# Cache copies and last intermediate stores of a transformer block, moved from GpSimd's DMA queue to ScalarE's and SyncE's

## The chip, the core and the metric

The kernel runs on one core of a Trainium2 chip. The core has TensorE (matrix products), VectorE, ScalarE and GpSimd (elementwise work), SyncE (which here only issues transfers), and DMA engines that move data between the chip's DRAM, the on-chip SBUF and so on. TensorE writes its products to PSUM, a small memory in banks from which the other engines drain them. Each engine takes its instructions from its own queue in order. A transfer is issued by an instruction in the queue of SyncE, ScalarE or GpSimd. The metric is device time in microseconds for one execution, as a median over runs; lower is better.

## The reference

The kernel computes one block of a network on 1056 tokens (1024 of a prompt, 32 of eight sampled sequences) of width 1024, in float32: a feed forward, a mixer (a convolution branch and a windowed attention with caches, merged by gates), and a second feed forward, each added to its input. Cut to what matters here:

```python
# D_MODEL 1024, D_FF 2816, L = 1
xp = xp + 0.5 * swiglu_ffn(rmsnorm(xp, ffn1_norm[l]), ffn1_w_in[l], ffn1_w_out[l])
...                                   # mixer: adds merge_branches(...)
xp = xp + 0.5 * swiglu_ffn(rmsnorm(xp, ffn2_norm[l]), ffn2_w_in[l], ffn2_w_out[l])
# the same for xs; for each of three windows, 128, 512 and 2048:
kf = jnp.concatenate([cache_k[g][l], ks[:, :, hsl]], axis=1)   # old rows, then four new ones
new_k_s[g].append(kf[:, kf.shape[1] - keep_s:])                # an output; the same for v
```

Outputs are the tokens, and the new caches. Most of a new cache is the old cache, shifted by the new rows, so a large part of the outputs is a plain copy from DRAM to DRAM.

## The kernel before

Activations lie transposed, with features on the partitions and tokens along the free axis. Each float32 product is taken in three TensorE passes over parts of 12 bits, so each operand is split in a high part (`wh`, a ScalarE copy, L170) and a low part (`wl`, the difference, by VectorE or GpSimd, L171). L164 to L172 hold this.

The second feed forward has two stages. In the hidden stage, the first two of 22 tiles of 128 hidden features are done plainly, and 20 by `hidden_fast`, which takes seven products of 24 matmuls each for one tile, in the Winograd form of Strassen's product. For one tile, SyncE loads two blocks of weights (`wr`), VectorE forms four sums of them (L433 to L436, into a `quad` buffer), each sum or block is split, and the seven products drain from PSUM into the same quad, by ScalarE (for instance L473, L476) or VectorE. There are four PSUM buffers for it, two per product. At a tile's end VectorE and ScalarE form the activation (L459, L462, L463), and `hidden_pair` follows: tiles 2i and 2i+1 are a pair, and for each of two token halves the kernel stores the operands that the second stage wants (combinations of the two tiles, by GpSimd, L517 and L522 to L524) to DRAM arrays `hx`. A quad is one of five buffers in a ring, so a later tile's sums wait until an earlier tile's store has been read out.

In the second stage, `ffn_out_fast` multiplies by the output weights, again in seven products for each of three groups of pairs; it loads weights (L563) and operands `hx` (L592), forms sums of weights (L569), and adds products to the tokens.

The order of instructions comes from two sources. The program has a clock that ticks once per block of matmuls; `later(n, fn)` has `fn` called n ticks on. Then a planner of the framework orders the instructions of each engine by a simulated machine. `keep_in_program_order` pins an instruction behind the one last traced on its engine.

`copy_caches` issues DRAM-to-DRAM copies of caches this way. Its part 0 (18 copies) is called in the first feed forward and issues from ScalarE. Its part 1 (17 copies) is called ahead of the second hidden stage with `COPY2 = (17, 7)`: the first copy comes 17 blocks of matmuls later, and then one each seven blocks, which is one per hidden tile. These are issued from GpSimd. No instruction waits for a copy's data. The stores of `hidden_pair` go out from SyncE, but for those of the last pair, four of them, which go out from GpSimd (`ENDQ = 1`).

Of the kernel before, what the change touches and what calls it, by code (L numbers as in the profile page):

```python
# [20 lines left out]
T = TP + TS  # L21
NB = 3
BW = T // NB
DFF = 2816
# [7 lines left out]
# which of the splits (by tile) VectorE takes, GpSimd the others  # L32
# [4 lines left out]
# places in the program, in blocks of matmuls: first, distance  # L37
# [4 lines left out]
ENDQ = 1  # L42
# [19 lines left out]
class Kern:  # L62
    """Activations are kept transposed (features on partitions, the 1056 tokens along the free axis). A float32 product
    x * w is taken in three float32r passes: x = xh + xl and w = wh + wl exactly, with 12 bits in each part."""
# [34 lines left out]
    def after(self, ins, first):  # L99
        """ins is issued after first (whose tile has its place by then)"""  # L100
        self.tc.add_manual_dep(ins.ins, first.ins.name, mybir.DependencyInfo(mybir.DependencyClass.NoSync, mybir.DependencyReason.DATA),
                               reason="order")

    def in_order(self, n0):
        """the instructions since n0 keep their order on each engine"""
        last = {}
        for i in self.nc.cur_bb.bb.instructions[n0:]:
            if i.engine == mybir.EngineType.SP:
                continue
            if i.engine in last:  # L110
                self.tc.add_manual_dep(i, last[i.engine].name, mybir.DependencyInfo(mybir.DependencyClass.NoSync, mybir.DependencyReason.DATA),
                                       reason="order")
            last[i.engine] = i
# [30 lines left out]
    def weights(self, src, kt, n, eng=None):  # L144
        """src: DRAM [kt*128, n] -> kt pairs (hi, lo) [128, n]"""
        nc = self.nc
        raw = self.P.tile([128, kt, n], F32, name=self.nm("wr"), tag="wr", bufs=3)
        nc.sync.dma_start(out=raw, in_=src.rearrange("(k p) n -> p k n", p=128))
        w = []
        for k in range(0, kt, 512 // n):  # L150
            m = min(512 // n, kt - k)
            hi = self.P.tile([128, m, n], F32R, name=self.nm("wh"), tag="wh", bufs=6)
            lo = self.P.tile([128, m, n], F32R, name=self.nm("wl"), tag="wl", bufs=6)
            nc.scalar.activation(hi, raw[:, k:k + m, :], AF.Copy)  # L154
            (eng or nc.gpsimd).tensor_tensor(out=lo, in0=raw[:, k:k + m, :], in1=f(hi), op=ALU.subtract)  # L155
            w += [(hi[:, j, :], lo[:, j, :]) for j in range(m)]
        return w

    def gemm(self, ps, w, xs, tb, tick=True):
        """ps[:, :BW] = sum_k w[k]^T xs[k][:, tb]"""  # L160
        nk = len(xs)
        for k, ((hi, lo), (xh, xl)) in enumerate(zip(w, xs)):
            for i, (p, x) in enumerate(((hi, xh), (hi, xl), (lo, xh))):
                self.nc.tensor.matmul(ps[:, :BW], p, x[:, blk(tb)],  # L164
                                      start=(k == 0 and i == 0), stop=(k == nk - 1 and i == 2))
        if tick:
            self.tick()
# [24 lines left out]
    def load_x(self, gname):  # L192
        """x^T (also to DRAM) and its norm, by blocks"""
# [85 lines left out]
    def norm_rows(self):  # L279
        """the normalized input of a feed forward, in float32 and split"""  # L280
        q = [self.quad() for _ in range(2)]
        self.hf = [q[k // 4][:, k % 4, :] for k in range(KT)]
        self.hs = [(self.hrow(), self.hrow()) for _ in range(KT)]
# [29 lines left out]
    def norm_feed(self, gname, k, tb):  # L313
        """after the last change of x^T's tile k in block tb; rbn gathers the squares' sums"""
        nc = self.nc
        if self.hn[k] is None:
            self.hn[k] = (self.hrow(), self.hrow())
        self.scaled(gname, k, tb, self.hn)
        self.square(k, tb)

    def norm_end(self, cols):
        """1/rms: rb over the tokens along the free axis, cols over tokens on partitions"""
# [16 lines left out]
    def hidden(self, w_in):  # L339
        """2 * silu(gate) * up -> self.hd, for 128 hidden features at a time"""  # L340
# [9 lines left out]
    def hidden_plain(self, g0, u0, g1, u1):  # L350
        """the first two tiles, from the normalized input as it comes by blocks"""
# [34 lines left out]
    # Winograd's form of Strassen's product, on [gate; up] x [first, second half of the features] and  # L386
    # [first, second half of the features] x [first, second half of the tokens]: 7 products in place of 8.
    #   S1 = A21 + A22   S2 = S1 - A11   S3 = A11 - A21   S4 = A12 - S2
    #   T1 = B12 - B11   T2 = B22 - T1   T3 = B22 - B12   T4 = T2 - B21
    #   P1 = A11 B11  P2 = A12 B21  P3 = S4 B22  P4 = A22 T4  P5 = S1 T1  P6 = S2 T2  P7 = S3 T3  # L390
    #   U2 = P1 + P6   U3 = U2 + P7   U4 = U2 + P5
    #   C11 = P1 + P2   C12 = U4 + P3   C21 = U3 - P4   C22 = U3 + P5
# [21 lines left out]
    def combine_last(self):  # L414
        """T4, in the place of B12"""
# [88 lines left out]
    # The same form for the output projection: [even, odd tiles of hidden features] x [first, second half of the tokens].  # L504
    # B11, T1, B21, B22, T3, T2, T4 of a pair of tiles go to self.hx.
# [3 lines left out]
    def hidden_pair(self, j, b, C):  # L509
# [10 lines left out]
        else:  # L520
# [4 lines left out]
            eng = nc.gpsimd if i >= DFF // 256 - ENDQ else nc.sync  # L525
            eng.dma_start(out=self.hx[i][1][:, :, sl], in_=C)
            eng.dma_start(out=self.hx[i][2][:, 0, sl], in_=k[:, b])

    def hidden_pair0(self, b):
        """from the two plain tiles"""  # L530
# [15 lines left out]
    def ffn_out_fast(self, w_out, final):  # L546
        """x^T += half of w_out^T hidden^T"""
# [9 lines left out]
        def load_w(c, q):  # L557
            """A11, A12, A21, A22: by two output tiles each"""
# [12 lines left out]
        def sums(c):  # L571
            """S2 in the place of A11, S1 in that of A21"""
# [7 lines left out]
        def last_sum(c):  # L580
            """S4, in the place of A12"""
            a = A[c]
            a["P3"] = a["P2"] if c < len(PAIRS) - 1 else block()
            combine(c, a["P3"], a["P2"], a["P6"], ALU.subtract)
# [85 lines left out]
    def ffn_out(self, w_out, after, begin=None):  # L670
        """x^T += half of w_out^T hidden^T, self.hd in chunks"""
# [39 lines left out]
    def store_y(self, o, h):  # L711
        """y for output tile o and half h of the tokens"""
# [52 lines left out]
    def u_unit(self, i):  # L765
        """u^T for 128 conv channels, and the conv's work on it, queued"""
# [29 lines left out]
        def states():  # L796
            # the last 32 prompt tokens and the sample tokens, for the conv states
# [6 lines left out]
            # sample tokens behind their states  # L804
# [31 lines left out]
    def conv_norm(self):  # L836
        """LayerNorm over channels and 2 * silu, split -> self.ca"""
# [62 lines left out]
    def gcols(self, row, g, i):  # L900
        """columns, in group g's order, of the prompt tokens 128 i + 0..127: by residue"""
# [11 lines left out]
    def keep(self, kind, g, i, src):  # L913
        """rows of k or v that are outputs"""
# [49 lines left out]
    def pack_sample(self):  # L964
        """the sample tokens' two parts, side by side"""
# [16 lines left out]
    def v_post(self, g, i, m, ps):  # L982
        """v in the order of the group's keys"""
# [74 lines left out]
    def attn_scores(self, g, i, keys, QT, KTt, V):  # L1058
# [6 lines left out]
        # the two heads of a pair on row tiles of their own, so in banks of their own  # L1065
# [56 lines left out]
    def merge(self, i):  # L1122
        """the three groups' parts, by their softmax sums -> b_attn^T"""
# [43 lines left out]
    def keep_sample(self, g):  # L1167
        """the sample tokens' q^T, k^T and v of this group"""
# [7 lines left out]
    def cached(self, kind, g, b):  # L1176
        """rows of the cached keys that the sample queries can read, 128 at a time"""
# [5 lines left out]
    def sample_scores(self, g, gap):  # L1183
        """scores of the rows (b, slot, s) -> self.SP: keys 0:512 group 1, 512:640 group 0, 640:768 group 2, 768:864 new"""
        nc = self.nc
        st = self.samp[g]
        # the queries of a sequence, block-diagonal over (sequence of a pair, slot)
# [130 lines left out]
    def copy_caches(self, part, t0, dt):  # L1318
# [14 lines left out]
        for n, (d, s) in enumerate(jobs[part::2]):  # L1333
            self.later(t0 + dt * n, lambda d=d, s=s: self.tc.keep_in_program_order((nc.gpsimd if part else nc.scalar).dma_start(out=d, in_=s)))

# [16 lines left out]
    def branches(self):  # L1352
        """4 * (sigmoid(gA) A + sigmoid(gB) B), split, in h's place"""
# [23 lines left out]
    def mix_out(self, mg):  # L1377
        """x^T += w_out^T (4 * merged)^T / 4, and its norm"""
# [113 lines left out]
def constants():  # L1492
# [7 lines left out]
    # sample rows (b, slot, s); keys: group 1 cache, group 0 cache, group 2 cache, new of groups 0, 1, 2  # L1500
# [44 lines left out]
```

## Time and profile before

| | us |
|---|---|
| Median of 3 runs | 2429.91 |
| Lowest and highest | 2428.36, 2432.47 |
| Profiled execution, span | 2432.6 |
| TensorE busy in it | 2314.0 (95%) |
| VectorE, ScalarE, GpSimd busy | 1501.7, 934.0, 1185.4 |

The profile is one execution. It gives the span from its first instruction to its last and no time of that execution beside it; the times of the runs come from other executions. In its rows PE is TensorE, PEld its weight loads, DVE VectorE, ACT ScalarE, POOL GpSimd and SP SyncE; ACTq and SPq mark transfers issued by an engine. L476 is line 476 of the kernel. The granted clock (PEclk) is the share of TensorE's full clock that it was granted: 1.00 is 2.4 GHz, and over a stretch in which it ran partly at 1.2 GHz the value lies between 0.5 and 1. The second hidden stage lies between 1700 and 2160 us of the span, and one pair of tiles takes some 47 us of it.

### The profile page before, as it was taken

Reading aid. Unit: us, or ns where it says so; the run is one execution under the profiler, and the core shown is the slowest. Engines: PE = TensorE matmul, PEld = TensorE weight load, DVE = VectorE, ACT = ScalarE, POOL = GpSimd, SP = SyncE. Lnnn points to the kernel's source line nnn. Section 1 sums busy time; section 2 is a strip of 40 time slices with the busy share of each in tenths; the row PEclk is TensorE's granted clock in tenths of the full one; section 3 lists DMA queues with packets and bytes.
Section 4 is the critical chain, followed back from the end, with each engine's and each line's share of the span. In section 5 each row is a group of like instructions: output and inputs, shape, how many; then the busy total and the mean of one; then the engine's idle time right before and its main releaser. Section 6 shows DMA issues by size and latency. Waiting matters only on the chain. (4 is left out here: it accounts for less than half of the span.)

```text
span 2432.6 us, 44152 instructions
## 1 busy us (share of the span) xinstructions
PE 2314.0 (95%) x16725; PEld 2248.6 (92%) x16725; DVE 1501.7 (62%) x2951; ACT 934.0 (38%) x2479; POOL 1185.4 (49%) x1148
## 2 busy tenths in 40 slices
PE   7899999999999999999999999988898998989998
PEld 6899999999999988987988999988898998989998
DVE  6777777752235545785667674248566566677765
ACT  4333333342125644544543252234333333334433
POOL 5744444443235413413412455456665655648685
PEclk8999999999999999999999999999999999999999
DMA  4322222274424111312343516522333323366223
GB/s 145 112 80 80 80 80 80 73 250 146 145 91 118 52 50 54 94 63 83 98 113 103 180 57 197 169 71 71 119 119 109 115 91 118 97 224 220 85 82 102
DMA packets 300185, 268.56 MB, mean 110 GB/s; under 512 B 21797, under 2 KB 281853, under 8 KB 299420
## 3 DMA queue, kind: packets, MB, share of 16 engines
q1 hardware_dynamic: 287052, 235.42, 31.1%
q10 hardware_dynamic: 11976, 19.60, 2.4%
q0 software_dynamic: 944, 10.72, 1.2%
q8 instruction: 131, 2.15, 0.4%
q14 instruction: 82, 0.67, 0.1%
HBM read 197.58 MB, written 87.27 MB: 117 GB/s over the span
## 5 line engine op out<-in xcount | busy, mean ns | idle before, releaser
L164 PE MATMUL mm<-h,wh 128*128 128x352 f32 x2448 | 623.2, 335 | 22.7 <-DVE h L171 9.2
L452 PE MATMUL mm<-h,wh 128*128 128x264 f32 x2560 | 475.2, 287 | 16.7 <-ACT wh L170 5.2
L164 PEld LDWEIGHTS mm<-h,wh 128*128 128x128 f32 x2448 | 438.5, 193 | 38.3 <-DVE h L171 11.6
L452 PEld LDWEIGHTS mm<-h,wh 128*128 128x128 f32 x2560 | 400.7, 190 | 18.0 <-ACT wh L170 5.7
L164 PE MATMUL mm<-h,wl 128*128 128x352 f32 x1224 | 405.3, 331 | 4.8 <-POOL wl L155 4.8
L452 PE MATMUL mm<-quad,wh 128*128 128x264 f32 x1920 | 364.8, 292 | 30.0 <-ACT quad L476 26.3
L452 PE MATMUL mm<-h,wl 128*128 128x264 f32 x1280 | 366.6, 286 | 3.0 <-POOL wl L171 3.0
L155 POOL TENSOR_TENSOR wl<-wr,wh 128x512 fp32r<-128x512 f32 (+2 forms) x160 | 198.9, 1257 | 310.6 <-ACT wh L154 266.6
L452 PEld LDWEIGHTS mm<-quad,wh 128*128 128x128 f32 x1920 | 307.3, 195 | 32.3 <-ACT quad L476 28.2
L171 POOL TENSOR_TENSOR wl<-quad,wh 128x512 fp32r<-128x512 f32 x160 | 219.7, 1376 | 202.5 <-ACT wh L170 175.9
L452 PE MATMUL mm<-quad,wl 128*128 128x264 f32 x960 | 275.2, 291 | 0.0
L628 PE MATMUL mm<-quad,wh 128*128 128x264 f32 x1232 | 235.9, 292 | 14.6 <-DVE quad L634 10.7
L452 PEld LDWEIGHTS mm<-h,wl 128*128 128x128 f32 x1280 | 243.1, 190 | 3.8 <-POOL wl L171 3.8
L164 PEld LDWEIGHTS mm<-h,wl 128*128 128x128 f32 x1224 | 236.9, 194 | 5.2 <-POOL wl L155 5.1
L953 PE MATMUL mm<-wh,h 128*128 128x256 f32 x1152 | 220.7, 287 | 0.0
L628 PEld LDWEIGHTS mm<-quad,wh 128*128 128x128 f32 x1232 | 196.9, 194 | 17.1 <-issue 9.5
L171 POOL TENSOR_TENSOR wl<-wr,wh 128x512 fp32r<-128x512 f32 x120 | 158.6, 1327 | 84.5 <-ACT wh L170 81.7
L452 PEld LDWEIGHTS mm<-quad,wl 128*128 128x128 f32 x960 | 185.6, 195 | 0.0
L953 PEld LDWEIGHTS mm<-wh,h 128*128 128x128 f32 x1152 | 181.5, 189 | 1.2 <-issue 0.6
L628 PE MATMUL mm<-quad,wl 128*128 128x264 f32 x616 | 178.5, 290 | 0.0
L459 DVE TENSOR_TENSOR quad<-quad 128x264 f32<-128x264 f32 x240 | 168.6, 703 | 10.9
L462 ACT ACTIVATE t<-quad 128x264 f32<-128x264 f32 x160 | 67.6, 423 | 270.6 <-DVE quad L459 270.6
(278 smaller groups left out, 4412.2 us busy)
## 6 DMA issues: line engine op xcount, KB each, us to landing
wr<-ffn_w_in SPq DMA_DIRECT2D x88, 512.0 KB
wr<-w_in SPq DMA_DIRECT2D x42, 512.0 KB
quad<-hx SPq DMA_DIRECT2D x74, 264.0 KB
quad<-xd SPq DMA_DIRECT2D x24, 528.0 KB
t<-hd SPq DMA_DIRECT2D x66, 176.0 KB
hd<-quad SPq DMA_DIRECT2D x40, 264.0 KB
hx<-quad SPq DMA_DIRECT2D x18, 528.0 KB
xd<-quad ACTq DMA_DIRECT2D x16, 528.0 KB
```

The lines of the kernel that those rows point to most:

```text
L155: (eng or nc.gpsimd).tensor_tensor(out=lo, in0=raw[:, k:k + m, :], in1=f(hi), op=ALU.subtract)
L164: self.nc.tensor.matmul(ps[:, :BW], p, x[:, blk(tb)], start=(k == 0 and i == 0), stop=(k == nk - 1 and i == 2))
L171: (eng or self.nc.vector).tensor_tensor(out=lo, in0=src, in1=f(hi), op=ALU.subtract)
L452: nc.tensor.matmul(ps[:, :HB], p[:, k, :], x[:, cols], start=(k == 0 and i == 0), stop=(k == 3 and i == 2))
L459: eng.tensor_tensor(out=out, in0=a, in1=b, op=op)
L462: nc.scalar.activation(t, C[b][:, c], AF.Tanh, scale=0.5)
L628: nc.tensor.matmul(ps[:, :HB], wp[:, k, :], q[:, s, k, cols], start=(k == 0 and i == 0), stop=(k == n - 1 and i == 2))
L953: nc.tensor.matmul(ps[:m, :256], x, w, start=(k == 0 and j == 0), stop=(k == 7 and j == 2))
```

## The change

All copies are issued from ScalarE, and all stores of `hidden_pair` from SyncE. What else the diff has is comments and docstrings, which are blanked so that the lines keep their numbers.

```diff
-ENDQ = 1
...
@@ hidden_pair
-            eng = nc.gpsimd if i >= DFF // 256 - ENDQ else nc.sync
-            eng.dma_start(out=self.hx[i][1][:, :, sl], in_=C)
-            eng.dma_start(out=self.hx[i][2][:, 0, sl], in_=k[:, b])
+            nc.sync.dma_start(out=self.hx[i][1][:, :, sl], in_=C)
+            nc.sync.dma_start(out=self.hx[i][2][:, 0, sl], in_=k[:, b])
...
@@ copy_caches
-            self.later(t0 + dt * n, lambda d=d, s=s: self.tc.keep_in_program_order((nc.gpsimd if part else nc.scalar).dma_start(out=d, in_=s)))
+            self.later(t0 + dt * n, lambda d=d, s=s: self.tc.keep_in_program_order(nc.scalar.dma_start(out=d, in_=s)))
```

## Rows read from the trace of the kernel before

**Rows 1.** The page: span, and busy time of each engine with its instructions.
```profile
span 2432.6 us, 44152 instructions
PE 2314.0 (95%) x16725; PEld 2248.6 (92%) x16725; DVE 1501.7 (62%) x2951; ACT 934.0 (38%) x2479; POOL 1185.4 (49%) x1148
```

**Rows 2.** TensorE's waits, 1820 to 2070: us in total, times, longest us.
```profile
PE mm L452 <- ACT quad L476: 22.3, 6, 3.9
```

**Rows 3.** Timeline of TensorE: start, us, operation, [idle before <-releaser].
```profile
1970.77 1.03 PE L452 MATMUL mm<-quad,wh 128*128 128x264 f32 x3 [3.84 <-ACT quad L476]
...
2113.06 0.52 PE L452 MATMUL mm<-quad,wh 128*128 128x264 f32 x2 [1.86 <-ACT quad L476]
...
2134.14 0.51 PE L452 MATMUL mm<-quad,wh 128*128 128x264 f32 x2 [0.39 <-ACT quad L476]
```

**Rows 4.** Windows: us, busy PE, PEld, DVE, ACT, POOL, then PEclk, DMA share, GB/s.
```profile
1828.60:1838.60 10.00, 9.97 (x69) 9.97 (x70) 6.09 (x14) 2.66 (x6) 4.27 (x4) 0.83 0.53 159
...
1970.70:1980.70 10.00, 9.93 (x60) 9.93 (x61) 5.05 (x11) 2.21 (x5) 4.37 (x4) 0.71 0.51 152
...
2066.00:2076.00 10.00, 9.95 (x59) 9.95 (x60) 4.98 (x11) 2.12 (x4) 4.41 (x4) 0.69 0.51 152
2113.00:2123.00 10.00, 9.94 (x81) 9.94 (x82) 9.05 (x16) 3.50 (x9) 6.79 (x6) 1.00 0.19 54
2180.90:2190.90 10.00, 9.95 (x66) 9.63 (x67) 10.00 (x13) 0.25 (x1) 1.25 (x1) 0.83 0.71 229
```

**Rows 5.** Timeline of GpSimd at a junction with a copy and one without.
```profile
1961.28 0.52 POOL L1334 DMA_DIRECT2D v_w_s<-cache_v_w  x1
1961.83 2.55 POOL L171 TENSOR_TENSOR wl<-quad,wh 128x512 fp32r<-128x512 f32 x2
1964.35 2.52 POOL L171 TENSOR_TENSOR wl<-wr,wh 128x512 fp32r<-128x512 f32 x2
...
2103.13 4.19 POOL L171 TENSOR_TENSOR wl<-quad,wh 128x512 fp32r<-128x512 f32 x3
```

**Rows 6.** Timeline of VectorE at the same two junctions.
```profile
1961.92 5.25 DVE L463 SCALAR_TENSOR_TENSOR quad<-t,quad 128x264 f32<-128x264 f32 x1 [2.12 <-ACT t L462]
...
2105.01 1.14 DVE L463 SCALAR_TENSOR_TENSOR quad<-t,quad 128x264 f32<-128x264 f32 x1 [2.12 <-ACT t L462]
...
2107.14 0.72 DVE L433 TENSOR_TENSOR quad<-wr 128x512 f32<-128x512 f32 x1 [0.98 <-DMA hx<-quad]
```

**Rows 7.** Timeline of ScalarE at the junction with a copy.
```profile
1960.11 0.42 ACT L518 ACTIVATE rb<-quad 128x264 f32<-128x264 f32 x1 [1.17 <-POOL quad L517]
...
1969.81 0.63 ACT L170 ACTIVATE wh<-quad 128x512 fp32r<-128x512 f32 x1 [6.06 <-DVE quad L435]
```

**Rows 8.** Line 1334, the copies: ns least/median/most, first and last start.
```profile
L1334 ACTq DMA_DIRECT2D k_w_s<-cache_k_w x9: 517/517/1320, 534.8 to 600.9; - x9
L1334 POOL DMA_DIRECT2D v_w_s<-cache_v_w x9: 524/527/608, 1883.4 to 2074.3; - x9
...
DMA to landing us min/median/max: 3.8/4.7/7.4
```

**Rows 9.** Window in the first feed forward, with copies issued from ScalarE (columns of rows 4).
```profile
560.00:600.00 40.00, 40.00 (x250) 40.00 (x249) 9.29 (x19) 8.75 (x19) 11.10 (x12) 1.00 0.47 149
```

**Rows 10.** Timelines of TensorE, GpSimd, VectorE and SyncE where the second stage begins.
```profile
2180.95 0.39 PE L628 MATMUL mm<-quad,wh 128*128 128x264 f32 x1 [2.41 <-POOL quad L171]
...
2178.31 0.73 POOL L526 DMA_DIRECT2D hx<-quad  x1
...
2179.54 2.61 POOL L171 TENSOR_TENSOR quad<-quad 128x528 fp32r<-128x528 f32 x2
...
2179.83 3.42 DVE L569 TENSOR_TENSOR h<-h,h 128x1024 f32<-128x1024 f32 x1
...
2164.68 4.99 SPq L563 DMA_DIRECT2D h<-ffn_w_out  x4
...
2185.27 0.32 SPq L592 DMA_DIRECT2D quad<-hd  x1
```

## The prediction

> **What bounds the kernel now.** I read the page's busy times first. TensorE is busy for 2314.0 of a span of 2432.6 us, no other engine for more than 62% of it [rows 1]. So time can come only from TensorE's idle gaps and from stretches in which it is busy at a low clock, and an edit counts by what it does to these two.
>
> Next I read TensorE's waits over the second hidden stage, where the copies lie. Between 1820 and 2070 us nearly all of them have one releaser: six waits for ScalarE's drain of a product out of PSUM (L476), 22.3 us together, the longest 3.9 [rows 2]. They come once for each pair of hidden tiles, where one pair ends and the next begins. One of them is the wait of 3.84 at 1970.77 [rows 3]. Behind each the granted clock is below 1: over the 10 us that follow, it is 0.83 at two junctions, 0.71 at two and 0.69 at two; a row of each kind stands in [rows 4]. The engine does the work of 8.3, 7.1 or 6.9 us in 10, so the loss is 1.7, 2.9 or 3.1, and 2 x (1.7 + 2.9 + 3.1) = 15.4 us over the six. Stalls and slow clock together are 22.3 + 15.4 = 37.7 us.
>
> Then I followed one stall back over the other engines' timelines. ScalarE stands still for 6.06 us before 1969.81, in a split (L170) that waits for VectorE's L435; L476 is queued behind that split, and TensorE waits for L476 because no PSUM buffer is free [rows 7]. VectorE is late because one small operation, L463 (128x264), takes 5.25 us from 1961.92 to 1967.17 [rows 6]. In the same microseconds GpSimd issues a cache copy at 1961.28, and behind it four splits without a gap, 1961.83 to 1966.87 [rows 5]. VectorE is let go 0.3 us after the last of them.
>
> One junction has no copy in it, since the 17 copies are used up at 2074.3 [rows 8]. There GpSimd again runs its splits without a gap, three in 4.19 us from 2103.13 [rows 5], yet L463 takes 1.14 us in place of 5.25, and VectorE's next operation waits 0.98 for the landing of a store of the pair that ends (hx<-quad) [rows 6]. TensorE waits 1.86, then 0.39 at the next product [rows 3], and keeps a clock of 1.00 [rows 4]. So what sets the long block is the pair: a DMA issued from GpSimd, and a run of GpSimd's splits close behind. It isn't so of every GpSimd DMA with a run behind it: near 2173 us, where the stores of the last pair's first half go out, VectorE is held only a little. So this is my reading of the six.
>
> **The change part by part.**
>
> A, the copies. 17 issues of 0.52 us [rows 8] leave GpSimd. GpSimd idles at these junctions once its run is done, so the 8.8 us of issue time are worth nothing by themselves. What they do to VectorE is worth something. For a junction after the change I take the one without a copy: 1.86 + 0.39 = 2.25 us, clock 1.00. That junction had no copy's packets beside its store either, and the copies still run. The store's landing is the next thing late, so I add what a transfer's landing differs by: copies land in 3.8, 4.7 and 7.4 us (least, median, most) [rows 8], so 0 at the least, 7.4 - 3.8 = 3.6 at the most, and I take median less least, 0.9, because the copies are spread one to a tile and meet a store by chance. A junction is then 3.15 us, six are 18.9, and A gains 37.7 - 18.9 = 18.8. The ends: at the most the stalls vanish, 37.7; with 3.6 at each, 6 x 5.85 = 35.1 are left and 2.6 gained. Where the block isn't the DMA's doing, the gain is below nothing (second rival).
>
> A's issues on ScalarE: 17 x 0.52 = 8.8 us on an engine with much idle time. The copy of a pair's first tile comes next to a place where ScalarE waits 1.17 us for GpSimd's L517 [rows 7], and that covers 0.52. The first half's copies are issued from ScalarE already, 0.517 each, and TensorE is busy 40.00 of 40 us with several of them in it, at a clock of 1.00 [rows 8, 9]. I cost them at nothing; without cover it is 8.8. No copy waits for data, so nothing is held behind one but its issue.
>
> B, the last four stores. GpSimd's two of the second half go out at 2178.31 and the splits behind them start at 2179.54: 1.23 us. TensorE waits 2.41 us for a later GpSimd split, to 2180.95, and its clock is 0.83 over the next 10 us [rows 4], a loss of 1.7. One of VectorE's sums (L569) takes 3.42 there, begun just behind the two issues [rows 10]. If the wait and the clock loss go, 2.41 + 1.7 = 4.1 us are gained; VectorE is busy for all 10.00 us of that window [rows 4], so it becomes the bound, and I take 3 of the 4.1. The ends are 0 and 4.1. On SP the four issues cost nothing: it stands idle ahead of its load at 2185.27 [rows 10], which itself reads what the stores write.
>
> Sum: 18.8 - 0 + 3 = 21.8 us, so a span of 2432.6 - 21.8 = 2410.8. The trace has no time for its execution beside the span, and the span is 2.7 above the median of the three runs, 2429.91. I take the same gain from the median: 2408.
>
> A rule that speaks against A is in the Trainium skill, "DMA: Bandwidth & Descriptors", section "Issuing engines are not separate DMA queues": transfers of every issuing engine share the same 16 DMA engines, and another issuer saves the issuing time alone. By it A would be 0, and the whole 1.2 of B's issue time, 2428.7. The six blocks speak against it here: they are time of VectorE, not of a transfer. It is the first rival's rule all the same.
>
> **The rivals.**
>
> First, the wait only moves. VectorE is free, but the store's landing, now with a copy issued from ScalarE into the same DMA engines, ends just as late: the lower end of A, 2.6 us, and nothing of B, as its loads wait on landings too. 2427. For it: VectorE did wait 0.98 for that landing as soon as the block was gone [rows 6]. Against it: at that junction the landing came 0.98 us after VectorE was ready, where the block holds it for 5.25.
>
> Second, slower: the block belongs to GpSimd's gapless run and not to the DMA. Then it stays at each of the six junctions, and ScalarE's 0.52 us stands ahead of L476 in the queue of the engine that TensorE waits for: 6 x 0.52 = 3.1, and the two junctions with a short stretch of slow clock get a long one, 2 x (3.1 - 1.7) = 2.8. B yields nothing, since VectorE stays blocked there too. 2429.9 + 5.9 = 2436. It decides if L463 still takes over 5 us with the copy elsewhere. For it: VectorE is let go just as the run ends [rows 5, 6]. Against it: the junction without a copy, with the same run. The Trainium skill, "SBUF — State Buffer", section "Who interferes with whom", says that VectorE and GpSimd lock a shared pair of ports for a whole instruction. By that rule one split, 1.3 us, is what VectorE waits; the 5.25 us across four splits agree only in that the two do block each other.
>
> Third, SP is held. The last stores wait for GpSimd's L524, which ends at about 2178.3. If they are put on SP ahead of the four weight loads that went out at 2164.68 [rows 10], these go out from 2178.3, take 4.99 us to issue and at least a copy's 3.8 to land: 2187.1. TensorE, ready at 2180.95 - 2.41 = 2178.54, waits 8.6 in place of 2.41, and loses up to 3.1 by the clock in place of 1.7: 7.6 us later. With A it comes to 18.8 - 7.6 = 11.2, 2419. For it: SP's order is drawn anew by a planner. Against it: the planner had the loads well ahead of stores that were late.
>
> **How the numbers follow.** My forecast has a chance of 0.66, the first rival 0.13, the second 0.11, the third 0.10. The forecast's own range goes from all of A without B, 2430 - 37.7 = 2392, to a junction with twice the landing term (6 x 4.05 = 24.3, gain 13.4), half of ScalarE's 8.8 and no B: 2430 - 9 = 2421. The range for all cases starts lower, at 2388, because A and B at their upper ends give 41.8, and reaches to 2429 over the first rival; the second rival and the odd tail, under 2 in 10, stay out. A measurement of this kernel can tell about 0.2%, 4.9 us, from no change. Faster than that are the forecast and the third rival, 0.76; the first rival and a little of the second are within it, 0.15; slower is most of the second, 0.09.
>
> **What would show it.** A is right if TensorE's six waits for L476 fall from 22.3 us to below 19 and their windows have a clock of 1.00, if no L463 or L433 on VectorE takes over 3 us in that stage, and if 17 copies more stand on ScalarE's queue. If the waits are short but the clock still falls, A is worth its idle part alone. The landing term is right if VectorE's waits for hx<-quad are the longest in their place, at 1 to 2 us. B is right if the wait for the split at the start of the second output product falls below 1 us and SP issues the four stores as GpSimd ends them, the last two at about 2178. Blocks of 5 us without a GpSimd DMA ahead of them would prove the second rival. A planner that draws another order in the whole stage, and so other junctions, would make the forecast wrong in either direction without touching its reading.

## The result and the profile after

The changed kernel takes 2399.18 us (median of 4 runs, 2394.41 to 2406.85) against 2429.14 (median of 4, 2426.61 to 2432.47): a ratio of 0.9877, 95% interval 0.9849 to 0.9905, so 30 us less. The forecast was 2408, its range 2388 to 2429. The sum came out near; two of its terms did not, and with opposite signs.

The page of the changed kernel, whose profiled execution took 2394.41 us, 1.8 more than its span. Its lines behind `ENDQ` (L42) are one less than before, those from the last stores of `hidden_pair` on two less.

```profile
span 2392.6 us, 44145 instructions
PE 2294.9 (96%) x16725; PEld 2228.9 (93%) x16725; DVE 1525.0 (64%) x2951; ACT 932.8 (39%) x2479; POOL 1177.0 (49%) x1127
```

The two profiles lie 40 us apart, 10 more than the medians: the one before lies above the median of its kernel, the one after is the shortest run of its own. I divide the span at TensorE's first and last matmul of the fast hidden tiles (L452 before, L451 after) and of the output products (L628, L626).

| us | before | after | difference |
|---|---|---|---|
| start to the first fast hidden tile | 1692.8 | 1685.3 | -7.6 |
| fast hidden tiles | 470.9 | 429.9 | -41.0 |
| output products | 262.4 | 271.1 | +8.7 |

The first row is not the change's: its code is the same, and in the kernels below, where it is the same too, that point lies anywhere between 1683.7 and 1692.5. The other two rows are the result. The hidden tiles gained more than all that I had put on their stalls, and the output stage lost. Of the 41.0 us, 36.9 lie in the six tiles that had the stalls and the tile behind each (285.0 before, 248.2 after), which is nearly the whole of the 37.7 that I had counted there; the rest lies in the first tiles and the last.

**The hidden tiles.** First, where the stalls lay. The prediction put them where one pair ends and the next begins. In the trace they lie inside a pair, in its second tile: what stands beside the wait at 1970.77 is the work on the end of a pair's first tile (L517 and L518 [rows 5, 7]), and the store that VectorE waited for in [rows 6] is that tile's, L519. A junction is that place in what follows. TensorE's waits from 1770 to 2100 us (total, times, longest), one of them on its timeline, and the windows behind two junctions:

```profile
PE mm L451 <- ACT quad L475: 1.8, 4, 0.6
```

```profile
1859.27 0.52 PE L451 MATMUL mm<-quad,wh 128*128 128x264 f32 x2 [0.55 <-ACT quad L475]
```

```profile
1859.20:1869.20 10.00, 9.94 (x81) 9.94 (x82) 8.50 (x16) 3.73 (x9) 5.85 (x6) 1.00 0.61 205
...
1941.60:1951.60 10.00, 9.77 (x80) 9.77 (x81) 8.65 (x17) 3.90 (x9) 5.82 (x6) 1.00 0.54 159
```

Against 22.3 us in six waits [rows 2] there are 1.8 in four, and the clock stays at 1.00 where it fell to 0.69 [rows 4]. A pair of those tiles takes 41.2 to 41.7 us where it took 46.4 to 48.0. The timelines of VectorE, ScalarE and TensorE in the tile that had the wait at 1970.77 show what took the block's place:

```profile
1934.12 0.43 DVE L462 SCALAR_TENSOR_TENSOR quad<-t,quad 128x264 f32<-128x264 f32 x1 [1.41 <-ACT t L461]
1935.94 0.69 DVE L432 TENSOR_TENSOR quad<-wr 128x512 f32<-128x512 f32 x1 [1.39 <-DMA hx<-quad]
...
1940.87 0.63 ACT L169 ACTIVATE wh<-quad 128x512 fp32r<-128x512 f32 x1 [4.39 <-DVE quad L434]
...
1941.84 0.52 PE L451 MATMUL mm<-quad,wh 128*128 128x264 f32 x2 [0.29 <-ACT quad L475]
```

No VectorE operation takes over 2 us in these tiles; L463 of before, here L462, takes 0.43 where it took 5.25 [rows 6]. VectorE now waits 1.39 us for the store's landing, more than the 0.98 of the old junction without a copy, and ScalarE waits 4.39 behind it where it waited 6.06 [rows 7]; TensorE loses 0.29. Between two pairs VectorE waits longer for a landing, up to 3.56, and TensorE has no wait there:

```profile
1917.67 1.37 DVE L432 TENSOR_TENSOR quad<-wr 128x512 f32<-128x512 f32 x1 [3.56 <-DMA hx<-quad]
```

All copies stand on ScalarE's queue (ns least, median, most, first and last start):

```profile
L1332 ACTq DMA_DIRECT2D k_w_s<-cache_k_w x17: 516/517/1327, 532.4 to 1839.8; - x17
...
L1332 ACTq DMA_DIRECT2D v_w_s<-cache_v_w x17: 516/517/735, 613.0 to 2026.0; - x17
```

GpSimd's order changed too, and the diff doesn't say so. The planner ordered the engines anew, and at a junction of the kind that stalled the order is (s4, s2, s3, s1 are splits of the sums, w those of a weight block, in the queue's order):

```
before: w  w  L517  s4  w  L517  s2  copy  s3  s1  w  w
after:  w  w  s4  w  s2  s3  L517  L517  s1  w  w
```

L517 has to wait for the first tile's end. In the old order it stands ahead of the splits of the second tile, so GpSimd idles at the first L517 and the splits gather behind it. Timeline of GpSimd before:

```profile
1954.71 1.83 POOL L517 TENSOR_TENSOR quad<-quad 128x264 f32<-128x264 f32 x1 [9.89 <-ACT rb L516]
```

**The output stage.** Timelines of SyncE, then of ScalarE, VectorE and TensorE:

```profile
2126.17 0.52 SPq L524 DMA_DIRECT2D hx<-quad  x1
2127.01 1.36 SPq L525 DMA_DIRECT2D hx<-rb  x1
2128.47 0.40 SPq L590 DMA_DIRECT2D quad<-hd  x1
...
2130.36 2.45 SPq L561 DMA_DIRECT2D h<-ffn_w_out  x4
...
2131.41 1.30 ACT L169 ACTIVATE quad<-quad 128x528 fp32r<-128x528 f32 x2 [4.09 <-DMA quad<-hd]
...
2132.11 0.59 PE L626 MATMUL mm<-quad,wh 128*128 128x264 f32 x1 [2.30 <-ACT quad L169]
...
2139.82 6.89 DVE L567 TENSOR_TENSOR h<-h,h 128x1024 f32<-128x1024 f32 x6
...
2147.11 0.51 PE L626 MATMUL mm<-quad,wh 128*128 128x264 f32 x2 [1.83 <-DVE quad L632]
...
2153.59 0.40 PE L626 MATMUL mm<-quad,wh 128*128 128x264 f32 x1 [1.86 <-POOL quad L170]
```

The stage starts at 2115.3. SyncE issues the last store at 2127.0, and only behind it the operand of the second product, 13.2 us into the stage; before, it issued that operand 4.5 us ahead of the stage. ScalarE waits 4.09 for the landing, TensorE 2.30 for ScalarE's split. That wait is no longer than the 2.41 of before [rows 10]; most of the loss comes behind it. The weights of L561 go out 15.1 us into the stage, where they went out 0.8 into it at 2164.68 [rows 10], and their sums begin 24.5 us into it, where they began 14.5 into it. Six sums in a row (6.89 us) hold VectorE's drains (L632) and TensorE behind them, and ScalarE stands 12.97 us for a sum, so the next operand's splits are late in turn. The third product begins 35.7 us into the stage, the fourth 51.4; before it was 30.6 and 44.0.

### The profile page after: what moved, and what is told of

It reads as the page before. It is cut to its first block, busy times and chain, and to the rows that moved or that the text cites. A ratio compares the mean times of both kernels' runs of the same rounds, so it can differ in the third digit from the quotient of the medians.

```text
span 2392.6 us, 44145 instructions
## 1 busy us (share of the span) xinstructions
PE 2294.9 (96%) x16725; PEld 2228.9 (93%) x16725; DVE 1525.0 (64%) x2951; ACT 932.8 (39%) x2479; POOL 1177.0 (49%) x1127
## 5 line engine op out<-in xcount | busy, mean ns | idle before, releaser
L451 PE MATMUL mm<-h,wh 128*128 128x264 f32 x2560 | 474.6, 286 | 12.3 <-DVE t L370 4.5
L451 PEld LDWEIGHTS mm<-h,wh 128*128 128x128 f32 x2560 | 400.2, 190 | 13.6 <-DVE t L370 4.9
L451 PE MATMUL mm<-h,wl 128*128 128x264 f32 x1280 | 365.2, 285 | 0.0
L451 PE MATMUL mm<-quad,wh 128*128 128x264 f32 x1920 | 356.1, 286 | 4.7 <-ACT quad L475 2.9
L170 POOL TENSOR_TENSOR wl<-quad,wh 128x512 fp32r<-128x512 f32 x160 | 223.5, 1398 | 231.2 <-ACT wh L169 209.8
L451 PEld LDWEIGHTS mm<-quad,wh 128*128 128x128 f32 x1920 | 299.1, 189 | 7.3 <-ACT quad L475 5.7
L451 PE MATMUL mm<-quad,wl 128*128 128x264 f32 x960 | 274.1, 286 | 4.6 <-POOL wl L170 4.6
L626 PE MATMUL mm<-quad,wh 128*128 128x264 f32 x1232 | 235.1, 291 | 22.2 <-DVE quad L632 13.3
L451 PEld LDWEIGHTS mm<-h,wl 128*128 128x128 f32 x1280 | 242.8, 190 | 0.0
L626 PEld LDWEIGHTS mm<-quad,wh 128*128 128x128 f32 x1232 | 194.7, 192 | 26.8 <-issue 9.7
L170 POOL TENSOR_TENSOR wl<-wr,wh 128x512 fp32r<-128x512 f32 x120 | 170.5, 1427 | 85.7 <-ACT wh L169 78.9
L458 DVE TENSOR_TENSOR quad<-quad 128x264 f32<-128x264 f32 x240 | 191.3, 802 | 12.3 <-DVE quad L458 0.5
L451 PEld LDWEIGHTS mm<-quad,wl 128*128 128x128 f32 x960 | 181.9, 189 | 4.9 <-POOL wl L170 4.9
L626 PE MATMUL mm<-quad,wl 128*128 128x264 f32 x616 | 177.1, 288 | 0.0
L153 ACT ACTIVATE wh<-wr 128x512 fp32r<-128x512 f32 x196 | 108.2, 574 | 162.5 <-PE mm L163 94.6
```

The costliest lines, as they stand in the source:

```text
L170: (eng or self.nc.vector).tensor_tensor(out=lo, in0=src, in1=f(hi), op=ALU.subtract)
L451: nc.tensor.matmul(ps[:, :HB], p[:, k, :], x[:, cols], start=(k == 0 and i == 0), stop=(k == 3 and i == 2))
L458: eng.tensor_tensor(out=out, in0=a, in1=b, op=op)
L626: nc.tensor.matmul(ps[:, :HB], wp[:, k, :], q[:, s, k, cols], start=(k == 0 and i == 0), stop=(k == n - 1 and i == 2))
```

## The experiments

Twelve kernels, each timed beside the kernel before, whose medians were 2428.97, 2429.73 and 2430.05 in the three sessions. "Hidden" and "output" are the stages of the table above, from each one's profile.

| kernel | us | ratio, 95% | hidden | output |
|---|---|---|---|---|
| e1, copies alone | 2386.69 | 0.9832 (0.9812 to 0.9852) | 431.9 | 262.1 |
| e2, stores alone | 2439.51 | 1.0039 (1.0025 to 1.0054) | 470.1 | 272.8 |
| e7, stores on ScalarE | 2398.60 | 0.9871 (0.9858 to 0.9885) | 431.1 | 268.8 |
| e3, no copies | 2387.74 | 0.9827 (0.9812 to 0.9842) | 429.4 | 259.3 |
| e4, 4 KB from GpSimd | 2391.65 | 0.9845 (0.9824 to 0.9866) | 432.9 | 262.7 |
| e5, memset | 2389.07 | 0.9839 (0.9818 to 0.9860) | 430.5 | 261.5 |
| e6, copies on SyncE | 2426.46 | 0.9983 (0.9970 to 0.9995) | 469.2 | 260.4 |
| e8, copies shifted | 2397.06 | 0.9866 (0.9839 to 0.9892) | 437.7 | 263.8 |
| h2, old order, memset | 2393.63 | 0.9846 (0.9829 to 0.9863) | 434.1 | 263.8 |
| h4, old order, 4 KB | 2396.89 | 0.9861 (0.9844 to 0.9877) | 440.1 | 261.5 |
| h3, old order, copy | 2416.94 | 0.9945 (0.9927 to 0.9964) | 459.5 | 260.0 |
| e9, copies later | 2378.26 | 0.9787 (0.9769 to 0.9804) | 422.8 | 262.3 |

**The two parts apart.** e1 has the new L1334 and the old stores, e2 the reverse, and e7 is e1 with the stores' engine swapped:

```diff
-            eng = nc.gpsimd if i >= DFF // 256 - ENDQ else nc.sync
+            eng = nc.scalar if i >= DFF // 256 - ENDQ else nc.sync
```

> Only the copies go to ScalarE; the last four stores stay on GpSimd. SyncE's order is that of the changed kernel but for these four stores. Theory (SyncE is held by the last stores, so that the operands and weights of the second and third output products go out late): the output stage is 271 us in the changed kernel and 262 before, so this one is some 9 us faster than the changed kernel, about 2390, and its output stage is 262 to 264. Rival (my prediction of the stores: they gain 3 us on SyncE): this one is 3 us slower than the changed kernel, about 2402.

> Only the last four stores go to SyncE; the copies stay on GpSimd. Theory (SyncE is held): the output stage gets some 9 us longer, 271 in place of 262, so about 2438, and the six stalls on ScalarE's L476 with VectorE blocks of 5 us are all still there. Rival (the stores gain 3 us as predicted): 2426.

> Copies on ScalarE and the last four stores on ScalarE as well, so neither GpSimd nor SyncE has them. Theory (what costs is that SyncE is held): no loads are late, and the output stage is 262 us or, as GpSimd's 1.2 us are gone too, up to 4 less: 2386 to 2390. Rival: ScalarE is held in its turn, as each store waits for GpSimd's L524 and splits and drains (L170, L630) stand behind it; then the output stage is 266 or more, 2394 and over.

The copies alone gain 42.3 us (2428.97 - 2386.69). The stores alone cost 10.5, and on top of the copies 12.5 (2399.18 - 2386.69). Timeline of e1, SyncE's second operand and weights, then the wait at the second product's start:

```profile
2110.22 0.41 SPq L592 DMA_DIRECT2D quad<-hd  x1
...
2115.56 5.18 SPq L563 DMA_DIRECT2D h<-ffn_w_out  x4
...
2131.82 0.39 PE L628 MATMUL mm<-quad,wh 128*128 128x264 f32 x1 [2.43 <-POOL quad L171]
```

They go out at 2110 and 2116, around the stage's start at 2115.9; GpSimd's stores and the wait of 2.43 are back as before [rows 10], and they cost less than what SyncE's order costs. In e2 TensorE's waits from 1820 to 2070 are those of before to the digit, and the operand is late again (waits, then timeline):

```profile
PE mm L452 <- ACT quad L476: 22.3, 6, 3.9
```

```profile
2169.01 0.53 SPq L527 DMA_DIRECT2D hx<-rb  x1
2169.63 0.73 SPq L592 DMA_DIRECT2D quad<-hd  x1
...
2173.70 0.39 PE L628 MATMUL mm<-quad,wh 128*128 128x264 f32 x1 [1.88 <-ACT quad L170]
```

In e7 the theory failed and the rival held. A queue that waits for a store's data holds whatever is behind it, on ScalarE too; VectorE's L634, which TensorE waits for, stands behind VectorE's own splits, and these wait for ScalarE's L170. Timeline of e7:

```profile
2130.64 0.59 ACTq L526 DMA_DIRECT2D hx<-quad  x1
2134.87 0.33 ACTq L527 DMA_DIRECT2D hx<-rb  x1
2135.24 2.24 ACT L170 ACTIVATE quad<-quad 128x528 fp32r<-128x528 f32 x4 [8.68 <-DMA hx<-rb]
...
2139.95 0.81 PE L628 MATMUL mm<-quad,wh 128*128 128x264 f32 x2 [9.61 <-DVE quad L634]
```

**What a copy costs off GpSimd.** e3 replaces L1480 by `pass`; e6 issues part 1 from `nc.sync`.

> The second half's 17 copies are left out (those outputs stay unwritten); the last stores stay on GpSimd. Theory (a copy on ScalarE costs nothing, neither by its issue nor by its traffic): the same as with the copies on ScalarE and the stores on GpSimd, about 2390, within 5 us. Rival (the traffic of the copies delays stores and weights, as I had 0.9 us at each of six junctions): 5 us or more faster than that, 2385 or less.

> The 17 copies on SyncE's queue, last stores on GpSimd. Theory (only GpSimd's queue is at fault, the other two have room): within 5 us of the copies on ScalarE, about 2390. Rival (a copy ahead of the weight loads on SyncE holds them up): 2400 or more, with VectorE's weight sums waiting for wr.

Leaving the copies out is no faster than issuing them from ScalarE (2387.74 and 2386.69), so issue and traffic cost nothing there that the medians can tell. The order differs between the two, though: in the profiles the two stages together are some 5 us shorter without copies, and e9 below, with all copies on ScalarE, is 9.5 us faster than e3. What order the planner draws weighs more than the copies. On SyncE nearly all of the gain is gone, and the rival held. VectorE's waits in e6, 1700 to 2150 us:

```profile
DVE quad L433 <- DMA wr<-ffn_w_in: 30.0, 6, 8.4
```

Its weight sums wait 30 us for weights (one such wait of 5.5 in before). In e1's order on SyncE, one load of the next tile stands ahead of a tile's stores, which wait for data; in e6, with the copies pinned between, both loads of a tile stand behind the stores of the one before. Timeline of SyncE in e6:

```profile
1932.62 0.34 SPq L527 DMA_DIRECT2D hx<-rb  x1
1933.05 0.39 SPq L427 DMA_DIRECT2D wr<-ffn_w_in  x1
1933.55 0.60 SPq L428 DMA_DIRECT2D wr<-ffn_w_in  x1
1934.19 0.93 SPq L1334 DMA_DIRECT2D v_w_s<-cache_v_w  x1
```

It is B's mechanism again; 17 issues, of 0.58 to 1.14 us each, don't make 40.

**Is it the DMA, the half microsecond, or the order?** e4 and e5 are e1 with one more GpSimd instruction beside each copy (one of the two lines marked):

```diff
+            if part:
+                self.later(t0 + dt * n, lambda n=n: self.tc.keep_in_program_order(nc.gpsimd.dma_start(out=self.scr[n], in_=a['ffn2_norm'][0].rearrange('(p c) -> p c', p=16))))   # e4
+                self.later(t0 + dt * n, lambda: self.tc.keep_in_program_order(nc.gpsimd.memset(self.fill, 0.0)))   # e5
```

> Copies on ScalarE, last stores on GpSimd, and beside each copy GpSimd issues a 4 KB transfer to scratch at the same place of the program (17 more transfers, read by nothing). Theory (a DMA issued from GpSimd with a run of splits close behind blocks VectorE, whatever it moves): blocks of 5 us on VectorE and stalls on L476 come back, 20 to 38 us, about 2415 to 2428. Rival (the block came from the copy's size or from the other order of instructions that the planner drew): as with copies on ScalarE alone, about 2390, and no VectorE operation over 3 us there.

> Copies on ScalarE, last stores on GpSimd, and beside each copy GpSimd does a memset of 128x512 (0.52 us in the trace of before, as long as the issue of a copy) into a scratch tile. Theory (the DMA blocks VectorE, not GpSimd's being busy half a microsecond more): about 2390, and no VectorE operation over 3 us in the hidden stage. Rival (any half microsecond more on GpSimd makes its run gapless, and the run blocks): stalls on L476 come back, 2415 or more.

> All as before, copies on GpSimd, but each copy three blocks of matmuls later (COPY2 = (20, 7)), so that it stands at another place of GpSimd's order. Theory (it blocks VectorE only where splits follow without a gap): the blocks of 5 us come where the copy lies ahead of such a run; at the new place, away from the tile's end, fewer or none, so 2392 to 2415. Rival (a copy on GpSimd costs wherever it stands, or the order of the whole stage decides): 2425 to 2435 as before.

e4 came out within 5 us of e1, so my theory as I had put it there was wrong in one word: 17 DMAs on GpSimd alone block nothing. They stood in places where no run of splits follows (GpSimd idles 3.7 or 4.0 us behind almost every one), so e4 tested no run, and e5 no more. e8 keeps the copies on GpSimd and gains 33 us by their place and the order that the planner draws with it. Its GpSimd and VectorE beside one copy:

```profile
2007.14 0.52 POOL L1334 DMA_DIRECT2D v_w_s<-cache_v_w  x1
2007.68 1.30 POOL L171 TENSOR_TENSOR wl<-wr,wh 128x512 fp32r<-128x512 f32 x1
...
2007.27 2.28 DVE L433 TENSOR_TENSOR quad<-wr 128x512 f32<-128x512 f32 x1 [1.93 <-POOL wl L171]
```

One split follows the copy, and VectorE's operation, 0.68 otherwise, takes 2.28 and is let go 0.6 after that split. That is the longest hold there, at three of the 17 copies (2.28 to 2.29 us); beside the others no VectorE operation takes over 1.9. With one split behind it, a copy makes no long block.

To separate DMA from order, h2, h4 and h3 pin GpSimd's old order at ten junctions; only X differs in the program, and in the fast hidden tiles h2 and h4 have the same order on GpSimd, VectorE, ScalarE and SyncE:

```diff
+                if n in (3, 5):      # s4, s2: behind the first, the second L517
+                    self.after(self.wl[-1], self.l517[n // 2 - 1])
+                if n == 5:           # X behind s2
+                    self.op = self.OP(j)
+                    self.after(self.op, self.wl[-1])
+                if n == 6:           # s3 behind X
+                    self.after(self.wl[-1], self.op)
```

> The second half's copies are left out, the last stores are on GpSimd. In every odd hidden tile from the fourth on, GpSimd is pinned to its order of before at a junction (split, L517, split, split, L517, split, X, four splits), and X is a memset of 128x512, 0.52 us. Two theories for the six stalls. D, the DMA ahead of the run holds VectorE: without a DMA no VectorE operation there is over 3 us, and each of the ten junctions costs about what the one without a copy cost before, 2.25 us, so some 10 x 1.8 above the kernel without copies (2387.7): 2400 to 2410. O, the order alone does it (L517 early, so four splits lie ready and run without a gap): blocks of 5 us on VectorE at all ten, each worth some 6.3 us, so 2435 to 2455.

> The same pinned order, copies left out, X is a 4 KB transfer issued from GpSimd into scratch, read by nothing. D: blocks of 5 us on VectorE behind each, ten stalls, 2435 to 2455, some 40 us above the one with the memset. O: as with the memset, whichever that is. If the copy's size is what matters, this one is like the memset and the one with whole rows is not.

> The same pinned order, X is a copy of one cache row of 512 KB issued from GpSimd, as in the kernel before; the other copies of the second half are left out. D and O both expect blocks of 5 us here and 2435 to 2455; it shows that the pinned order with such a copy is the case of before, and against the 4 KB transfer what the size does.

The same junction in h2 and in h4, GpSimd, then VectorE, then TensorE:

```profile
1936.72 0.52 POOL L1493 MEMSET fill<- 128x512 f32 x1
1937.21 2.76 POOL L171 TENSOR_TENSOR wl<-quad,wh 128x512 fp32r<-128x512 f32 x2
1939.93 3.43 POOL L171 TENSOR_TENSOR wl<-wr,wh 128x512 fp32r<-128x512 f32 x2
...
1937.90 0.90 DVE L473 SCALAR_TENSOR_TENSOR quad<-t,quad 128x264 f32<-128x264 f32 x1 [0.49 <-ACT t L472]
1939.79 0.72 DVE L433 TENSOR_TENSOR quad<-wr 128x512 f32<-128x512 f32 x1 [0.99 <-DMA hx<-quad]
...
1945.71 0.51 PE L462 MATMUL mm<-quad,wh 128*128 128x264 f32 x2 [0.83 <-ACT quad L486]
```

```profile
1940.44 0.53 POOL L1493 DMA_DIRECT2D scr<-ffn_norm  x1
1940.99 2.57 POOL L171 TENSOR_TENSOR wl<-quad,wh 128x512 fp32r<-128x512 f32 x2
1943.52 2.53 POOL L171 TENSOR_TENSOR wl<-wr,wh 128x512 fp32r<-128x512 f32 x2
...
1941.61 4.73 DVE L473 SCALAR_TENSOR_TENSOR quad<-t,quad 128x264 f32<-128x264 f32 x1 [0.49 <-ACT t L472]
...
1949.95 0.51 PE L462 MATMUL mm<-quad,wh 128*128 128x264 f32 x2 [1.36 <-ACT quad L486]
```

L473 here is L463 of before. It begins 1.2 us after X in both. Behind a memset it gets in between two splits and takes 0.90; behind a DMA, of 4 KB and with nobody waiting for it, it is held for 4.73, to the end of the fourth split. That is theory D, at all ten junctions (2.23 at the last, where only two splits follow), and the order alone makes no block. But D's price was wrong: the block is worth 3.3 us over the ten (2396.89 - 2393.63; 6.0 by the hidden tiles of the two profiles), not 40, and all three kernels ran faster than forecast. Here is h3, with a copy of 512 KB as X (timeline of VectorE and TensorE, then the window behind):

```profile
1955.33 4.73 DVE L473 SCALAR_TENSOR_TENSOR quad<-t,quad 128x264 f32<-128x264 f32 x1 [0.49 <-ACT t L472]
...
1963.67 1.00 PE L462 MATMUL mm<-quad,wh 128*128 128x264 f32 x6 [2.57 <-ACT quad L486]
```

```profile
1963.60:1973.60 10.00, 9.93 (x69) 9.93 (x70) 6.22 (x13) 2.62 (x6) 5.36 (x4) 0.83 0.36 107
```

The block is the same, the wait 2.57 in place of 1.36, the clock 0.83 (1.00 in h4), the whole 20 us longer. From the block's end to TensorE's restart it is 3.6 us in before, h4 and h3 alike (1967.17 to 1970.77, 1946.34 to 1949.95, 1960.06 to 1963.67). What differs is when TensorE runs dry: 0.2 us before the block's end in before, 1.0 behind it in h3, 2.25 in h4. So a block costs what exceeds TensorE's lead, that is the work it still has while VectorE is held, and more where the clock falls behind the stall (0.83 behind 2.57 us, 1.00 behind 1.36). Why the lead is less with a large copy stays open: in h3 the planner also swapped a few operations of VectorE and ScalarE in each pair, and the copy has its traffic; the runs don't part the two. Nor do the three rebuild the whole loss. The twelve tiles of the six old junctions take 248.0 us in e1, 256.3 in h2, 258.8 in h4, 269.8 in h3 and 285.0 in before; what makes the last 15.2, between h3 and before, no run here shows.

**A faster version.** e9 is e1 with `COPY2 = (24, 7)`. In e1 TensorE meets this in the first fast tile, which takes 33.5 us (before 24.8):

```profile
1709.72 0.59 PE L452 MATMUL mm<-quad,wl 128*128 128x264 f32 x1 [5.15 <-POOL wl L171]
```

> All copies on ScalarE, last stores on GpSimd, as in the fastest so far, but the first copy seven blocks of matmuls later (COPY2 = (24, 7)). In the fastest so far the first fast hidden tile takes 33.5 us, with a wait of 5.15 for a GpSimd split behind work on the first pair (L536); the kernel without copies has another order there and takes 26.3. Theory (the first pinned copy draws that order): the first tile takes 26 to 27 here, and the whole is some 7 us faster than 2386.7, about 2380. Rival (that order comes from elsewhere, or the time goes to the next tiles): within 3 us of 2387.

The first tile takes 26.3, the others stay at 20.4 to 21.4 but for the last, and the kernel runs at 2378.26: 52 us below before (2430.05), 20.9 below the changed kernel.

## Why the prediction was right, and where it wasn't

- "The change part by part", A: the forecast of less stall by moving copies off GpSimd held, and the reading behind it, a GpSimd DMA with splits close behind holds VectorE, is shown by h2 against h4. The term was mis-sized: 18.8 forecast, 42.3 measured (e1), over its upper end of 37.7. In e1's profile the twelve tiles of the six junctions give 37.0 of it, so there nearly all of the stalls and of the slow clock went; the rest lies outside them, where the term had nothing. I took a junction after the change as the old one without a copy, 2.25 us, plus 0.9 for a landing. It measures 0.3 to 0.8 us for most pairs (a tile with a junction 20.75 to 21.24 us, without one 20.42). That old junction had L517 early in GpSimd's queue, and the planner moved it once the copy was gone. h2 pins it back, without a DMA, and a pair costs 42.6 us there, 1.8 over 2 x 20.42, against 0.8 over in e3, without copies or pins; so about 1 of the 2.25 was the order. The hold's own price is small where the order is pinned (h4 against h2), so the reading named a cause of the stalls and not all of it. I had named the planner as a danger and given it no sign and no term.
- A's landing term: at five of the six junctions VectorE waits 1.38 to 1.47 us for hx<-quad, within my 1 to 2; but TensorE waits 1.3 us over all six, so the 0.9 at each that I had added was not lost.
- A's issues on ScalarE at nothing: right as far as the medians tell; e3 and e1 agree within 1.1 us.
- B failed: +3 forecast, -12.5 measured (-10.5 by e2). The step was "On SP the four issues cost nothing: it stands idle ahead of its load at 2185.27". It looked at SyncE's idle time before and not at what the planner would queue behind the stores. The third rival had the mechanism; it named the weights of L563 at 2164.68, and priced it at 7.6 us. What was late first was the second operand (L592), then those weights; and the wait that it lengthened, 2.41 to 8.6 at the second product, stayed at 2.30, while the time was lost behind it. I gave it 0.10.
- The first rival, that the wait only moves to the landing, fails by its price. VectorE's wait did move: its waits for hx<-quad rise from 4.5 us in three to 26.6 in 14; TensorE's didn't. The rule beside it ("DMA: Bandwidth & Descriptors", "Issuing engines are not separate DMA queues", of the Trainium skill), that another issuer saves the issuing time alone, doesn't hold here: e1 gains 42, and e6 and e1 differ by 40 us by the issuing queue and the order that comes with it.
- The second rival fails: no block of 5 us is left with the copies elsewhere. Its rule of the Trainium skill ("SBUF — State Buffer", "Who interferes with whom"), a lock for one instruction, agrees with h2, where L473 waits part of one split. It doesn't tell of h4, where the hold goes over four.

So it was luck that the time came near: A's surplus of 23.5 us covered B's deficit of 15.5. The sign of A was not luck.

## What to carry to other kernels

Look at each queue as a list in order: an issue that waits for data held what was behind it on SyncE and on ScalarE alike (e2, e7), so ask what stands behind it, not whether the engine is idle. A pinned instruction also moves the planner's order, which can be worth more than the instruction; measure its place (e8, e9) before its engine. And a blocked helper engine costs only what exceeds the lead that the bounding engine still has, plus what its clock loses behind the stall.

## What the runs showed of the hardware that was not expected

At the junctions a VectorE operation on two SBUF tiles (L463 or L433 in before, L473 in h3 and h4) that starts behind a DMA issued from GpSimd is held to the end of the gapless GpSimd run that follows: 4.7 to 5.8 us for four splits, 2.23 for two, with 4 KB as with 512 KB; behind a memset of the same length it waits for part of one split (0.90 in all). GpSimd's splits keep their pace of 1.27 to 1.3 us in the first case and stretch to 1.7 in the second. It isn't so behind every such DMA: near 2173 us in before, two such operations (L171) pass in 0.81 and 1.27 us while GpSimd works on without a gap. What parts the two cases stays open.
